# First visits of a token write its output row with the residual, second visits add to it

## The chip, the cores and the metric

The kernel runs on one core of one Trainium2 chip. The metric is the device time of one execution in microseconds (us). The kernel before took 811.41 us, the median of three runs (808.11 to 816.99). One execution of it was profiled; every row shown below comes from that one.

## The reference

One decoder layer on 1024 tokens of width 1024. The first half (attention, a linear recurrence, an output projection) gives the residual stream x. The second half routes each token to two of 32 experts, and the layer's output is x plus the gated sum of what these two experts give:

```
x  = x + gate1 * (mixed @ w_out)
h2 = rms_norm(x, norm2_g) * (1.0 + scale2) + shift2
g_p, g_idx = lax.top_k(g_prob, 1)                       # 1 of 4 groups
e_p, e_idx = lax.top_k(softmax(e_logits), TOP_K)        # 2 of its 8 experts
hid = silu(xb @ w_gate[e]) * (xb @ w_up[e])             # xb: the tokens of expert e
y   = zeros.at[row_tok].add((hid @ w_down[e]) * row_w)  # two rows are added per token
x   = x + gate2 * y
```

## The kernel before

The kernel is one program for all five engines; a scheduler puts each engine's instructions into a fixed order, in which they then run. The change touches the second half, from about 440 us of the 814.6 us span on.

**Routing.** For each pair of 128-token tiles `route` (L1273) finds the two experts of each token, and `places` (L1319) counts each token's place in its expert's list (`slot`). It turns places into lists with a product of one-hot matrices: `rec` holds for each token and choice its number and its weight, `ohs` the one-hot of the place, and `ptab` the result, a table of 32 experts by 128 places, summed up in `tb`. `h2_rows` (L1235) does two things for a tile of tokens: it writes the residual rows to the result with a DMA from the POOL queue (L1238, `out<-xr`), and the normed rows to a scratch tensor in HBM, `h2_d` (L1247).

**Units.** The expert work is cut into 20 units of up to 128 rows (`UNITS`, L73), filled in steps of 32 rows from the lists of one to four experts. Eight experts, two of each group, are fixed in advance ("front"): units 0 to 4 use only these, so their weights can be loaded before the routing is known. The other experts are ranked by their counts, and the ranking (`permi`) names the weights to load. Experts with more than 128 tokens have second and third pieces, which only units 10, 11, 14, 15 and 16 use. Lists of first pieces come from `tb`, resorted by rank (`tki`, `tkw`, L1501 to L1512); lists of further pieces come from a later pass, `overflow_tables` (L1519), which runs in small steps between the units. `pack` copies the pieces of a unit into one column of row numbers (`pki`) and weights (`pkw`).

**One unit.** For unit n the main loop (L1678) issues the loads of new experts, then the gather for unit n + 2; `gate_up` (L1642) multiplies, and in its middle the rows of unit n + 1 are transposed (`xpose`, L1604, `pxe` to `xeT`); `act` (L1620) makes `hid`; `hid_t` transposes it (`pht`, `hT`); `down` (L1653) multiplies by the third weight matrix (`py`), VectorE multiplies by `gate2` into `y` (L1663), and an indirect DMA from the POOL queue adds the rows of `y` to the rows of the result in HBM (L1665, `out<-y`, an accumulating transfer).

**Buffers and queues.** Gathered rows go to `NX` = 2 buffers (`xe`), used in turn: the gather of unit n + 2 waits until the transposes of unit n have read theirs. Expert weights are tiles of 512 KB, six per expert, 186 in all, loaded by the SP queue (L1125) into a pool of `NBLK` = 41 buffers that also holds the gate row `m_g`; a load waits for a free buffer, and for the load four places before it (`fly`). All DMA queues share the core's 16 DMA engines.

Of the kernel before, what the change touches and what calls it, by code (L numbers as in the profile page):

```python
# [26 lines left out]
NBLK = 41  # L27
BACC = dict(dynamic_dma_scratch_size=4096)
NX = 2
# [13 lines left out]
ROWS = [("gqp", 64), ("gkp", 64), ("freq", 32), ("br", 36)]  # L43
# [15 lines left out]
EBASE = {8: 1, 9: 4, 10: 7}  # L59
NST = 8  # L60
NOV = NST + 32

# [33 lines left out]
MULTI = [u for u in UNITS if len(u) > 1]  # L96
NFU = 5
GRP = [("same", 32), ("in", 4), ("by", 4), ("base", 1), ("full", 32), ("shift", 32)]
GOFF = {}
_o = 0  # L100
for _n, _w in GRP:
# [15 lines left out]
    "pt": "VS", "gl0": 6, "xa": 3, "pf": {31: 4, 32: 3, 22: 1, 25: 1, 28: 3, 7: 2, 11: 4, 12: 8, 16: 1, 17: 30}, "sqA": "G", "mg": 61, "h2p": "SSSSSSSS", "xp": "SSSSVVVV", "rh": "G", "hk": 7, "sep": 0, "rw": 2, "glw": 54, "mL": "V", "k1": 3, "gs": 1, "adv": 1, "adv0": 0, "fly": 4, "fly0": 4, "lo": "VVVG", "ptc": "SSV", "lw": 1, "lw2": 1, "lw3": 2, "lw4": 3, "ro": 0, "in_l1": "G", "xsc": "VSVSVVVV", "pin": "Y", "st": 0, "ta": 2, "sq": "SSVVSSVV", "sqL": "G",  # L117
# [21 lines left out]
def layer(ctx, tc, A, out, dbg=None, stop=None):  # L139
# [193 lines left out]
    V.tensor_scalar(tokm, tokc[:, :NT], -float(S), None, op0=OP.add)  # L333
# [840 lines left out]
    NXE = 2  # L1174
# [26 lines left out]
    rec = c2.tile([128, NT, 2, 2], F32, name="rec")  # L1201
    tb = c2.tile([128, 64], F32, name="tb")
# [32 lines left out]
    def h2_rows(t):  # L1235
        x1 = St[t]["x"]
        tsl = slice(t * 128, t * 128 + 128)
        G.dma_start(out[tsl, :], x1)  # L1238
# [80 lines left out]
    def places(g):  # L1319
# [3 lines left out]
        for a in range(2):  # L1323
            o = pp[:, a * 32:a * 32 + 32]
            T.matmul(o, tri, mb[:, a], start=True, stop=False)
            if a:
# [6 lines left out]
        V.scalar_tensor_tensor(rec[:, ts, :, 0], slot[:, ts], -1.0, tokm[:, ts, None].to_broadcast([128, 2, 2]),  # L1333
                               op0=OP.mult, op1=OP.add)
        ptab = bank("ptab")[:, :64]
        tc_ = "p t c a -> p (t c) a"
        rh = sm.tile([128, 4, 2, 32], F32, name="rhs", bufs=1)
        V.tensor_mul(rh, M[:, ts].rearrange(tc_)[:, :, None, :].to_broadcast([128, 4, 2, 32]),
                     rec[:, ts].rearrange(tc_)[:, :, :, None].to_broadcast([128, 4, 2, 32]))
        for c in range(2):  # L1340
# [3 lines left out]
            for a in range(2):  # L1344
                T.matmul(ptab, oh[:, a], rh[:, 2 * a + c].rearrange("p c e -> p (c e)"), start=(c == 0 and a == 0),
                         stop=(c == 1 and a == 1))
# [80 lines left out]
    trash = tokc[:, NT:NT + 1]  # L1427
    tk0 = c2.tile([128, 32], I32, name="tk0")
    V.tensor_scalar(tk0, tb[:, 0:32], trash, None, op0=OP.add)
# [11 lines left out]
    def column(p, m):  # L1441
        if p < NF:
            e = FRONT[p]
            return tk0[:, e:e + 1], tb[:, 32 + e:33 + e]
        if m:
            c = EBASE[p] + m - 1
            return toi[:, c:c + 1], tow[:, c:c + 1]
        return tki[:, p:p + 1], tkw[:, p:p + 1]

    def plan(u):  # L1450
        if len(u) == 1:
            i, w = column(*u[0][:2])
        else:
            c = MULTI.index(u)
            i, w = pki[:, c:c + 1], pkw[:, c:c + 1]
        n = max(g[2] + g[3] for g in u) * 32
        return i[:n], w[:n], [(0, i[:n])]

    pki = c2.tile([128, len(MULTI)], I32, name="pki")
    pkw = c2.tile([128, len(MULTI)], F32, name="pkw")  # L1460
    xrow = {0: gather(plan(UNITS[0])[0])}

    def pack(pieces):
        for c, (p, m, a, n, r) in pieces:
            i, w = column(p, m)
            V.tensor_copy(pki[32 * a:32 * (a + n), c:c + 1], i[r:r + 32 * n])
            last["pack"] = V.tensor_copy(pkw[32 * a:32 * (a + n), c:c + 1], w[r:r + 32 * n]).ins
# [210 lines left out]
    for n, u in enumerate(UNITS):  # L1678
# [4 lines left out]
        if n + 2 < len(UNITS):  # L1683
            if any(g[1] for g in UNITS[n + 2]):
                drain(tab)
# [89 lines left out]
```

## Time and profile before

| | |
|---|---|
| runs | 808.11, 811.41, 816.99 us, median 811.41 |
| profiled execution, its own time | 816.49 us |
| its span, first to last instruction | 814.6 us |
| TensorE (PE) busy | 728.1 us (89%) |
| VectorE (DVE) busy | 447.2 us (55%) |
| ScalarE (ACT) busy | 317.0 us (39%) |
| GpSimd (POOL) busy | 157.6 us (19%) |
| moved by DMA | 180.47 MB |
| expert weight loads | 186 of 512 KB, the last issued at 792.0 us |
| first product of the expert stage, last scatter | 520.5 us, 806.85 us |

The profile says of each engine when it was busy, what it waited for, and how busy the 16 DMA engines were. An engine with little idle time is not by that alone the bound: one has to see for whom the others wait in each stretch. The chain of waits in this trace holds only the last scatter and no more, so it does not answer that; the stretches do.

### The profile page before, as it was taken

The page shows a single profiled execution, that of the slowest core. Times are in us where ns is not written, and L with a number is a line of the kernel's source. Part 1 is how long each engine was busy: PE and PEld are TensorE (multiplying, and loading weights), DVE is VectorE, ACT ScalarE, POOL GpSimd, SP SyncE. Part 2 cuts the span into 40 slices and gives each one's busy share as a digit, 9 for nine tenths or more (in the row PEclk, how much of TensorE's full clock was granted, in tenths as well). Part 3 has the DMA queues.
Part 4 walks back from the last instruction along what each step waited for, and adds up shares of the span by engine and source line. Part 5 has one row for each costly group of instructions (what it writes and reads, how often), then busy time and mean ns, then how long its engine had stood idle before and what let it go on. Part 6 is the DMA issues. An engine that isn't in the chain of part 4 may idle for free. (4 is left out here: it accounts for less than half of the span.)

```text
span 814.6 us, 12260 instructions
## 1 busy us (share of the span) xinstructions
PE 728.1 (89%) x4257; PEld 471.2 (58%) x4257; DVE 447.2 (55%) x1334; ACT 317.0 (39%) x715; POOL 157.6 (19%) x150
## 2 busy tenths in 40 slices
PE   3899999989988989899999997699979899999874
PEld 1477776548877878788888886333333343332321
DVE  4597386868777469797884667344334222213210
ACT  3455456666354157667664434121201211102200
POOL 1121012103665102031311000212112112212010
PEclk9989999999999999999999998699989999999998
DMA  9952437681317403020154789999999999999994
GB/s 311 372 151 84 143 108 236 210 280 58 109 44 259 168 39 104 1 79 1 54 173 144 259 311 343 346 316 349 313 373 330 329 335 336 369 347 354 304 320 102
DMA packets 70976, 180.47 MB, mean 222 GB/s; under 512 B 8960, under 2 KB 22528, under 8 KB 70912
## 3 DMA queue, kind: packets, MB, share of 16 engines
q1 hardware_dynamic: 63328, 158.50, 55.1%
q0 software_dynamic: 7104, 21.00, 9.5%
q8 instruction: 34, 0.56, 0.3%
q10 hardware_dynamic: 480, 0.16, 0.2%
q14 instruction: 30, 0.25, 0.1%
HBM read 160.61 MB, written 22.95 MB: 225 GB/s over the span
## 5 line engine op out<-in xcount | busy, mean ns | idle before, releaser
L1649 PE MATMUL pgu<-ew,xeT 128*32 128x512 f32 (+1 forms) x928 | 163.4, 613 | 8.1 <-DMA ew<-in_w_e 7.3
L1649 PEld LDWEIGHTS pgu<-ew,xeT 128*32 128x32 f32 (+1 forms) x928 | 48.3, 121 | 99.4 <-issue 79.0
L1660 PE MATMUL py<-ew,hT 128*32 128x512 f32 (+1 forms) x464 | 75.1, 597 | 5.8 <-ACT hT L1634 5.8
L225 PE MATMUL pp<-hTh,winh 128*128 128x512 f32 x176 | 69.2, 406 | 5.8 <-DVE hTh L188 3.0
L226 PE MATMUL pp<-hTl,winh 128*128 128x512 f32 x176 | 71.1, 404 | 0.0
L227 PE MATMUL pp<-hTh,winl 128*128 128x512 f32 x176 | 70.4, 401 | 0.0
L1663 DVE TENSOR_TENSOR y<-py,m_g 128x512 f32<-128x512 f32 (+1 forms) x40 | 27.5, 691 | 69.3 <-PE py L1660 64.3
L1623 ACT ACTIVATE sg<-pgu 128x256 f32<-128x256 f32 (+1 forms) x20 | 7.7, 387 | 142.9 <-PE pgu L1649 135.8
L1660 PEld LDWEIGHTS py<-ew,hT 128*32 128x32 f32 (+1 forms) x464 | 23.5, 120 | 48.3 <-issue 35.7
L1616 DVE TENSOR_SCALAR xeT<-pxe,gc,mc 128x128 f32<-128x128 f32 x80 | 27.4, 404 | 33.0 <-PE pxe L1610 33.0
L225 PEld LDWEIGHTS pp<-hTh,winh 128*128 128x128 f32 x176 | 34.0, 194 | 16.3 <-DVE hTh L188 4.0
L1665 POOL DMA_INDIRECT out<-y,pki x13 | 20.7, 1589 | 111.2 <-DVE y L1663 87.7
L1625 DVE SCALAR_TENSOR_TENSOR hid<-sg,pkw,pgu 128x256 f32<-128x256 f32 (+1 forms) x13 | 6.2, 479 | 63.4 <-ACT sg L1623 60.9
L1634 ACT ACTIVATE hT<-pht 128x256 f32<-128x256 f32 (+1 forms) x20 | 7.6, 380 | 85.1 <-PE pht L1632 65.4
L1614 ACT ACTIVATE xeT<-pxe,mc,gc 128x128 f32<-128x128 f32 x80 | 30.0, 461 | 24.9 <-PE pxe L1610 24.9
L226 PEld LDWEIGHTS pp<-hTl,winh 128*128 128x128 f32 x176 | 33.9, 193 | 9.9 <-issue 2.1
L227 PEld LDWEIGHTS pp<-hTh,winl 128*128 128x128 f32 x176 | 34.1, 194 | 8.6 <-issue 1.7
L949 ACT ACTIVATE P<-pS,nb,scq 128x384 f32<-128x384 f32 (+2 forms) x48 | 32.3, 679 | 12.2 <-DVE nb L946 12.2
L983 PE MATMUL po<-PT,v 128*128 128x256 f32 (+1 forms) x160 | 35.8, 362 | 0.0
L1046 POOL TENSOR_TENSOR wo<-wo,m_g 128x256 f32<-128x256 f32 x32 | 28.2, 916 | 15.3 <-DMA wo<-in_w_out 15.3
L983 PEld LDWEIGHTS po<-PT,v 128*128 128x128 f32 x160 | 28.8, 191 | 2.9
L1610 PEld LDWEIGHTS pxe<-ident,xe 128*128 128x128 f32 x160 | 18.2, 145 | 20.7 <-issue 14.4
(424 smaller groups left out, 1613.6 us busy)
## 6 DMA issues: line engine op xcount, KB each, us to landing
ew<-in_w_e SPq DMA_DIRECT2D x186, 512.0 KB
wad<-in_w_ada SPq DMA_DIRECT2D x64, 256.0 KB
wada<-in_w_ada SPq DMA_DIRECT2D x16, 512.0 KB
win<-in_w_in SPq DMA_DIRECT2D x12, 512.0 KB
xt<-in_x SPq DMA_DIRECT2D x8, 512.0 KB
wo<-in_w_out SPq DMA_DIRECT2D x8, 512.0 KB
xr<-in_x SPq DMA_DIRECT2D x8, 512.0 KB
x_d<-xr SPq DMA_DIRECT2D x8, 512.0 KB
```

Of the source, the lines that this page charges most:

```text
L225: T.matmul(o, lhi, rhi, start=first, stop=False)
L226: T.matmul(o, lhi, rlo, start=False, stop=False)
L227: T.matmul(o, llo, rhi, start=False, stop=last)
L949: SC.activation(Pt[:, o:o + w], pss[ci], AF.Exp, scale=P["scq"][:, i:i + 1], bias=nb, accum_out=l[:, ci:ci + 1])
L983: T.matmul(po[:, o:], P["v"][:, js], PT[j // 4][:, j % 4, o:], start=(j == 0), stop=(j == nj - 1), skip_group_check=True)
L1046: EN[OPT["g1"]].tensor_mul(w[:, q:q + 256], w[:, q:q + 256], mrow["g1"][:, q:q + 256])
L1614: SC.activation(xT[a][:, c], pt[:, c], AF.Identity, scale=gc[:, k:k + 1], bias=sh2[:, k:k + 1])
L1616: last["dve"] = V.tensor_scalar(xT[a][:, c], pt[:, c], gc[:, k:k + 1], sh2[:, k:k + 1], op0=OP.mult, op1=OP.add).ins
L1649: T.matmul(pg[r], xT[k // 4][:, c + r.start:c + r.stop], w[k // 2][:, NS[k % 2]], start=(k == 0), stop=(k == 7), skip_group_check=True)
L1660: T.matmul(py[n][r], hT[:, a * 128 + r.start:a * 128 + r.stop], w[4 + a][:, NS[n]], start=(a == 0), stop=(a == 1), skip_group_check=True)
L1663: last["dve"] = V.tensor_mul(y[:rows, NS[n]], py[n][:rows], mrow["g2"][:rows, NS[n]]).ins
L1665: G.indirect_dma_start(out=out, out_offset=bass.IndirectOffsetOnAxis(ap=idx, axis=0), in_=y[r0:r0 + idx.shape[0]], in_offset=None, compute ...
```

## The change

Every token is visited twice. The new kernel marks for each of its two rows whether it is the earlier one in the order of the units. The earlier row is written to the result by a plain scatter, with the residual already added to it; the later one is added by an accumulating scatter.

- The eight writes of the residual (L1238) are gone. Instead `down` adds the residual to `y`: the gathered row is x times its norm factor, so x is that row times the reciprocal of the factor (`rinv`). The third value of `rec` is that reciprocal for a first visit and 0 for a second, and one more vector operation per half of `y` (L1696 of the new file) uses it.
- Each unit has three lists in place of one: `get` for the gather, `put` and `add` for the two scatters, made by four small operations (`lists`). A row that does not belong to a scatter has a number outside the result and is skipped. Unit 0 has only a `put`. The two scatters go to two views of the result that the scheduler treats as different tensors; each `add` waits for the `put` of the unit before.
- Since `y` now reads the gathered rows, their buffer is held until then: `NX` is 3, and `NBLK` is 40 in return.
- Only the front experts get their lists in `places` (8 columns of three values in place of 32 of two; four more small vector operations per pair of tiles decide who is first). The resorting (L1501 to L1512) is gone. All other units, from unit 5 on, take their lists from one late pass, `late_tables`, which is the former overflow pass with 64 columns of three values; it runs in units 0 to 2, three steps at a time, and must be done before the gather of unit 5.

```
-NBLK = 41
+NBLK = 40
-NX = 2
+NX = 3
...
     def h2_rows(t):
-        G.dma_start(out[tsl, :], x1)
...
+        V.tensor_tensor(inc, pp3, RW("cff")[:, None, :].to_broadcast([128, 2, 32]), op=OP.is_lt)
+        V.tensor_mul(scr, inc[:, :, None, :].to_broadcast([128, 2, 2, 32]), M[:, ts])
+        fst = two(2, "fst")
+        V.tensor_reduce(fst, scr, op=OP.add, axis=AX.X)
+        V.reciprocal(rinv[:, ts], ivx[:, ts])
+        V.tensor_mul(fst, fst, rinv[:, ts, None].to_broadcast([128, 2, 2]))
+        for c in range(2):
+            V.tensor_sub(rec[:, ts, c, 2], rinv[:, ts], fst[:, :, 1 - c])
...
+    def lists(c0, c1, src=None, dst=None):
...
+        V.tensor_scalar(get, v[:, :, 0], float(OOB), None, op0=OP.add)
+        V.tensor_scalar(t, v[:, :, 2], 0.0, 2.0 * OOB, op0=OP.is_gt, op1=OP.mult)
+        V.scalar_tensor_tensor(put, v[:, :, 0], 3.0 * OOB, t, op0=OP.add, op1=OP.subtract)
+        last["pack"] = V.scalar_tensor_tensor(add, v[:, :, 0], float(OOB), t, op0=OP.add, op1=OP.add).ins
...
-    pT = bank("pT")
-    for c in range(2):
-        T.transpose(pT[:32, c * 128:c * 128 + 128], tb[:, c * 32:c * 32 + 32], ident)
...
     def late_tables():
...
+        for c in range(2):
+            for t0 in range(0, NT, 2):
+                ts = slice(t0, t0 + 2)
+                oh = t3(half("oh")[:, :256], 2)
+                V.tensor_tensor(oh, iota[:, None, :].to_broadcast([128, 2, 128]),
+                                pf[:, ts, c:c + 1].to_broadcast([128, 2, 128]), op=OP.is_equal)
+                rh = half("rh")[:, :384].rearrange("p (t v e) -> p t v e", t=2, v=3)
...
+                if ready:
+                    products(*ready)
...
         for n in range(2):
-            last["dve"] = V.tensor_mul(y[:rows, NS[n]], py[n][:rows], mrow["g2"][:rows, NS[n]]).ins
...
+            V.tensor_mul(y[:rows, NS[n]], py[n][:rows], mrow["g2"][:rows, NS[n]])
+            last["dve"] = V.scalar_tensor_tensor(y[:rows, NS[n]], x[:rows, NS[n]], r, y[:rows, NS[n]],
+                                                 op0=OP.mult, op1=OP.add).ins
...
+            before = last.get("put")
+            last["put"] = scatter(seen[0], put, OP.bypass)
+            if add is not None:
+                i = scatter(seen[1], add, OP.add)
+                tc.add_manual_dep(i, before.name, mybir.DependencyInfo(
+                    mybir.DependencyClass.Sync, mybir.DependencyReason.DATA), reason="rows are written before they are added to")
...
         if n + 2 < len(UNITS):
+            while n + 2 >= NFU and done[0] < n + 3:
+                next(tab)
+            xrow[n + 2] = gather(plan(n + 2)[0])
```

The order of the instructions moves at three places of which the prediction speaks. The first is the POOL queue at the start of the expert stage. Before, the gathers (`xe<-h_d`) of units 0 to 4 stand ahead of the first scatter, then scatter and gather take turns:

```order
L1437 DMA xe<-h_d,tk_5370 128x1024
L1437 DMA xe<-h_d,pki 128x1024 x4
L1665 DMA out<-y,tk_5370 1024x1024
L1437 DMA xe<-h_d,pki 128x1024
L1665 DMA out<-y,pki 1024x1024
L1437 DMA xe<-h_d,pki 128x1024
```

In the changed kernel:

```order
L1460 DMA xe<-h_d,idx_get 128x1024 x3
L1700 DMA out<-y,idx_put 1024x1024
L1460 DMA xe<-h_d,idx_get 128x1024
L1700 DMA out<-y,idx_put 1024x1024
L1700 DMA out<-y,idx_add 1024x1024
L1460 DMA xe<-h_d,idx_get 128x1024
```

Three gathers stand ahead of the first scatter; from there on the gather of unit m stands behind the scatters of unit m - 3.

The second place is PE from the down product of unit 0 (`py`, 128x512) to that of unit 1. Before, the transposes for unit 2 (`pxe`, 7 and 1) stand here, and those for unit 3 come later:

```order
L1660 MATMUL py_5533<-ew,hT 128x512
L1649 MATMUL pgu<-ew,xeT 32x512 x17
L1610 MATMUL pxe<-ident,xe 128x128 x7
L1632 MATMUL pht<-ident,hid 128x128 x2
L1610 MATMUL pxe<-ident,xe 128x128
L1649 MATMUL pgu<-ew,xeT 32x512 x16
L1660 MATMUL py<-ew,hT 32x512 x4
```

In the changed kernel:

```order
L1692 MATMUL py_5591<-ew,hT 128x512
L1678 MATMUL pgu<-ew,xeT 32x512 x32
L1639 MATMUL pxe<-ident,xe 128x128 x8
L1661 MATMUL pht<-ident,hid 128x128 x2
L1692 MATMUL py<-ew,hT 32x512 x4
L1692 MATMUL py_5737<-ew,hT 32x512 x4
```

These eight transposes are those of unit 3. They stand ahead of the down product of unit 1, so that product waits for the gather of unit 3 too.

The third place is VectorE, from the `y` of unit 0 to the `hid` of unit 1. Before, it holds short copies of lists between them:

```order
L1663 TENSOR_TENSOR y<-py_5533,m_g_5155 128x512
L1466 COPY pki<-tki 64x1
L1467 COPY pkw<-tkw 64x1
L1466 COPY pki<-tki 32x1
L1467 COPY pkw<-tkw 32x1
```

In the changed kernel the two new operations of `y` and the late pass (`mt`, `o_...`) stand ahead of the scaled transposes of unit 2 (`xeT`):

```order
L1696 SCALAR_TENSOR_TENSOR y<-xe,pk,y 128x512
L1695 TENSOR_TENSOR y<-py_5591,m_g_5173 128x512
L1696 SCALAR_TENSOR_TENSOR y<-xe,pk,y 128x512
L1571 TENSOR_TENSOR mt<-M,fs 128x256 x3
L1645 TENSOR_SCALAR xeT<-pxe,gc,mc_349 128x128 x4
L1575 TENSOR_TENSOR o_full<-slot,o_full 128x16
L1572 TENSOR_REDUCE o_shift<-mt 128x8
```

The late pass has moved two units ahead: before, its first rows come behind the `y` of unit 1.

## Rows read from the trace of the kernel before

**Rows 1.** The page: busy tenths of the DMA engines in 40 slices.

```profile
DMA  9952437681317403020154789999999999999994
```

**Rows 2.** Stretches: PE, PEld, DVE, ACT, POOL busy; PEclk, DMA share, GB/s.

```profile
440.00:480.00 40.00, 40.00 (x239) 35.00 (x238) 22.07 (x116) 18.00 (x43) 2.93 (x5) 1.00 0.64 219
480.00:520.00 40.00, 27.62 (x187) 24.34 (x187) 25.81 (x160) 12.68 (x31) 3.70 (x5) 0.81 0.98 369
520.00:560.00 40.00, 40.00 (x274) 15.61 (x276) 15.46 (x78) 8.96 (x22) 8.25 (x7) 0.98 0.94 318
560.00:600.00 40.00, 36.62 (x297) 12.70 (x290) 18.06 (x55) 6.38 (x18) 8.00 (x7) 1.00 0.97 334
680.00:720.00 40.00, 37.02 (x199) 13.75 (x198) 10.89 (x23) 6.32 (x18) 8.67 (x7) 1.00 1.02 358
```

**Rows 3.** What the SP queue waited for, 520 to 537 us: total, times, longest.

```profile
SPq L1125 <- PE pgu L1649: 9.7, 6, 2.9
```

**Rows 4.** The same from 537 to 795 us.

```profile
SPq L1125 <- DMA ew<-in_w_e: 166.9, 135, 4.2
SPq L1125 <- PE pgu L1649: 3.5, 13, 0.4
```

**Rows 5.** Weight loads from 520 us on: count, durations in ns, first and last start.

```profile
L1125 SPq DMA_DIRECT2D ew<-in_w_e x146: 327/333/762, 523.1 to 792.0; - x146
L1125 SPq MOVE ew<-in_w_e x138: 29/29/37, 538.4 to 791.9; - x138
```

**Rows 6.** POOL's DMA queue, 480 to 509 us: packets, MB, share of 16 engines.

```profile
q0 software_dynamic: 432, 1.57, 13.3%
...
out<-xr POOLq DMA_DIRECT2D x3, 512.0 KB, 7.5
```

**Rows 7.** The same queue from 756 to 796 us.

```profile
q0 software_dynamic: 533, 1.70, 23.0%
```

**Rows 8.** Another queue, on the page, with packets of about 340 bytes.

```profile
q10 hardware_dynamic: 480, 0.16, 0.2%
```

**Rows 9.** Gathers: ns min/median/max on POOL; us from issue to landing.

```profile
L1437 POOL DMA_INDIRECT xe<-h_d,pki x13: 989/1029/1060, 512.0 to 746.5; - x13
...
DMA to landing us min/median/max: 7.7/8.0/9.9
```

**Rows 10.** Scatters on POOL, the same columns.

```profile
L1665 POOL DMA_INDIRECT out<-y,pki x13: 1475/1592/1792, 554.8 to 806.8; - x13
```

**Rows 11.** PE in order of time: start, us, instruction, count.

```profile
537.39 3.70 PE L1660 MATMUL py<-ew,hT 128*128 128x512 f32 x8
541.02 4.48 PE L1649 MATMUL pgu<-ew,xeT 128*32 128x512 f32 x34
...
550.13 3.62 PE L1660 MATMUL py<-ew,hT 128*32 128x512 f32 x32
...
563.27 3.64 PE L1660 MATMUL py<-ew,hT 128*32 128x512 f32 x32 [0.47 <-ACT hT L1634]
...
606.83 3.72 PE L1660 MATMUL py<-ew,hT 128*32 128x512 f32 x32
...
802.05 3.64 PE L1660 MATMUL py<-ew,hT 128*32 128x512 f32 x32 [0.47 <-ACT hT L1634]
```

**Rows 12.** DVE and POOL behind the last down product, in order of time.

```profile
804.92 1.52 DVE L1663 TENSOR_TENSOR y<-py,m_g 128x512 f32<-128x512 f32 x2 [3.84 <-PE py L1660]
...
806.85 1.55 POOL L1665 DMA_INDIRECT out<-y,pki  x1 [17.09 <-DVE y L1663]
```

**Rows 13.** DVE by line, 500 to 815 us: busy, mean ns, idle before.

```profile
L1663 DVE TENSOR_TENSOR y<-py,m_g 128x512 f32<-128x512 f32 x38 | 26.2, 692 | 66.0 <-PE py L1660 61.0 <-issue 4.3 <-PE pgu L1649 0.2
```

**Rows 14.** PE by line, 597 to 622 us, the same columns.

```profile
L1589 PE MATMUL pto<-ov 128*128 128x80 f32 x32 | 4.7, 302 | 2.9 <-DVE ov L1586 2.9
```

**Rows 15.** VectorE and POOL at the start of the expert stage.

```profile
510.04 0.24 DVE L1429 TENSOR_SCALAR tk<-tb,tokc 128x32 int32<-128x32 f32 x1
...
510.56 1.08 POOL L1437 DMA_INDIRECT xe<-h_d,tk  x1 [12.39 <-DVE tk L1429]
```

## What the prediction says

> **What bounds the kernel now.** I read the page's slices first, then a table of stretches, then the waits of the queue that issues the weight loads, and last PE in order of time. From 480 us almost to the end the DMA engines are full [rows 1, 2]; PE is as busy as they are only up to unit 5. So there are two candidates. The SP queue tells them apart. From 520 to 537 us its loads wait mostly for `pgu` on PE [rows 3], which means that all 41 buffers are full and PE sets the pace. From 537 to 795 us they wait 166.9 us for an earlier load and 3.5 us for PE [rows 4]: the loads run as fast as the DMA engines let them. 138 loads of ranked experts are issued from 538.4 to 791.9 us [rows 5], 253.5/138 = 1.84 us each. The last down product `py` ends at 802.05 + 3.64 = 805.69 us [rows 11], 13.7 us after the last load is issued.
>
> PE has a pace of its own that is a little faster. Its `py` ends at 541.09, 553.75 and 566.91 us [rows 11]: 12.7 and 13.2 us per unit, 12.9 in the mean. From unit 5 (`py` ends at 610.55 us) to unit 19 (805.69 us) it needs 195.14/14 = 13.94 us. The gap, 1.0 us in each of 14 units, is what the transfers hold PE up by, and all that the change can give back by relieving them.
>
> The sums below are made against the profiled run: a span of 814.6 us, 816.5 us in all. It lies 0.6% above the median of 811.41, so I multiply its totals by 811.41/816.49 = 0.9938.
>
> **What the transfers gain.** Half of the 2048 visits write plainly where before they added. Nothing in the trace writes rows plainly by an index; the nearest are the plain rows on POOL's queue, residual writes and gathers, from 480 to 509 us: 13.3% of 16 engines for 29 us are 61.7 us, over 384 rows of 4 KB 0.161 us of one engine per row [rows 6]. Where adding scatters stand beside a gather, 23.0% of 16 × 40 us are 147 us over 415 rows (1.70 MB), 0.355 us a row [rows 7]. The difference, 0.194 us × 1024 rows / 16 engines, is 12.4 us, from nothing (a put costs as much as an add) to 12.4; I take 12.4, since a put has the form of the plain rows.
>
> The eight residual writes vanish. Three of them lie in the full stretch [rows 6]: 384 × 0.161/16 = 3.9 us. I count them at nothing, because buffers are full right behind it [rows 3] and earlier loads would only wait there; the bound is −3.9. The other five lie in a stretch whose DMA share is 0.64 [rows 2], where other transfers have room. Rows that are skipped, some 2,400 more of them, are not seen apart in this trace. The cheapest packets on another queue take 0.2% × 814.6 × 16/480 = 0.054 us [rows 8]; the bounds are 0 and 2400 × 0.054/16 = 8 us, and I take 2, because a skipped row carries no data. One buffer fewer starts each load one load later: 0 to 1.84 us [rows 5], taken whole.
>
> **What the gathers lose.** This is the term against the change. `y` now reads `xe`, so the gather of unit m is released by `y` of unit m − 3 and not by transposes, and it stands on POOL behind that unit's put and add. From the end of `py(m − 3)`: 2.0 us for four operations of about 0.7, the first of which runs beside the product [rows 12, 13], 0.5 to reach POOL, the put 1.0 to 1.6 (a gather takes 1.03, a scatter 1.59 [rows 9, 10]; I take 1.3), the add 1.6, 0.6 between them, and 8.0 to land (7.7 to 9.9 [rows 9]). That is 14.0 us, from 13.4 to 16.2. Then PE may transpose unit m, and the end of `py(m − 1)` follows 12.9 us behind. So two units take at least 26.9 us, 13.45 each. In about half of the units some products stand between `py` and the transposes, which covers about 1 us of the gather and makes it 12.9. The loop runs at 13.2 us per unit, from 12.9 to 14.5. The DMA engines would allow 13.94 − (12.4 − 2)/16 = 13.3, and PE 12.9. I take 13.2.
>
> **Up to unit 5.** Before, five gathers went out ahead of all scatters and waited for nothing that was late. Now
> - the first gather is behind about six more small vector operations at 0.24 us [rows 15]: +1.4 (0 to 2.4);
> - the late pass stands on VectorE ahead of `hid` and `xeT` in units 0 to 2: +2 in unit 0 (0 to 3), from three `mt` and their like at 0.24 to 0.7 each [rows 13, 15];
> - the transposes of unit 3 stand ahead of `py(1)`. With `py(0)` at about 541.1 + 3.4 = 544.5 us, its gather is issued near 549 and lands near 557, while PE would be there at 549 to 553: +5 (4 to 8);
> - the gathers of units 4 and 5, in the same loop: +3 (0 to 6). In that wait lie the products of the tables, 4.7 us before [rows 14], now 192 columns wide in place of 80; without this cover they would cost up to 4.7 × 192/80 = 11.3 us.
>
> Together +11.4 us: `py(5)` ends near 622. The cover for the whole of this is nil, PE being busy all the time there [rows 2].
>
> **Behind the last product.** Two more operations of `y` and a second scatter in place of one. Before, the span ends 8.9 us after `py`: `y`, the issue of the scatter at 806.85 us [rows 12], and its landing. Two operations at about 0.7 less what overlaps, 1.3, and an issue of 1.6 with 0.3 between: +3.2 us. No cover: nothing else runs there.
>
> **The sum.** 610.55 + 11.4 + 14 × 13.2 = 806.8 us, against 805.7 before: +1.1. With the tail +4.3: 820.8 us for the profiled run's 816.5, or 816 on the scale of the median. What 12.4 us of transfers give back, the gathers take.
>
> **The rivals.**
> *Faster: the transfers decide.* If the gathers land early enough (7.7 us and less, as with fewer rows and a shorter queue), and PE's late start is made up from the full buffers, the end follows the last load: −12.4 + 2 + 1.8 + 1.4 + 3.2 = −4.0 us, 807.5 on the median; with the residual writes and no cost of skipped rows or of the start −12.4 − 3.9 + 1.8 + 3.2 = −11.3, 800. For it: the SP queue waits for transfers through 258 us [rows 4]. Against: PE has only 1.0 us per unit to make up 11.4 with. It decides if the loop stays under 13 us and the start under 6.
>
> *Slower: the loop of gathers binds in every unit.* Landing of 9 us and more, as the longest before [rows 9], gives (15 + 12.9)/2 = 13.9 us in each unit: 623.8 + 14 × 13.9 = 818.4, +12.7, with the tail +15.9, 827 on the median. Its place is POOL's queue, where a gather is third behind two scatters. For it: the DMA engines are full where it lands [rows 2], and it now lands beside two scatters. Against: a put is shorter than an add. It decides from a landing of about 9 us on.
>
> *The change does not do what it says.* A put costs as much as an add [rows 7], nothing is relieved, and the units keep 13.9 us: in the loads' sum 2 + 1.8 + 1.4 + 3.2 = +8.4, 820 on the median.
>
> *POOL is held up by VectorE.* The new `y` operation reads two operands in SBUF while POOL prepares scatters and gathers. Between 554.8 and 611 us scatters were issued beside such vector operations of the tables and took no more than 1.79 us [rows 10], so no row here speaks for it; if an issue took 3 us instead of 1.6, the loop would gain 4 us in two units, 15.4 us each, and the kernel 30 us.
> The Trainium skill, "SBUF — State Buffer", section "SBUF: two separate sides", states such a lock: a VectorE operation with two SBUF inputs and a GpSimd operation that reads SBUF exclude each other for the whole instruction, and a transfer issued from GpSimd can starve for its descriptors behind a VectorE copy. By that page the loss would be larger still, 620 ns becoming about 3100 (its section "A bandwidth-pool intuition that's wrong"), but the trace so far does not agree with it for these forms.
>
> **How the numbers follow.** The forecast has 0.43, the faster rival 0.27, the loop 0.24, the puts without gain 0.03, VectorE's hold 0.03. The forecast's own range is 808 (start +6, pace 13.0) to 822 (start +15, pace 13.4). About 1% is what a measurement of this kernel can tell from no change: faster is below 803.3, slower above 819.5. Of the faster rival's two ends one lies on either side of 803.3, so I put half of it, with a little of the forecast, below: 0.15. Slower are most of the loop's 0.24 (0.21), the upper end of the forecast (0.05) and most of the last two (0.04): 0.30. The rest, 0.55, is the same. The range goes from 802, between the two ends of the faster rival, to 829, a little past the loop's 827, and leaves about 1 in 10 out on either side.
>
> **What would show it.** Right: the waits of the SP queue behind 537 us move from earlier loads to `pgu` on PE; the last load is issued earlier than 792 us while `py(19)` is not; PE's `pxe` waits for transfers of `xe`, some 5 us at unit 3 near 550 to 558 us; `py(5)` ends near 622 us; the pace behind it is near 13.2 us; POOL's queue shows less than 0.355 us per row late in the stage; the span ends about 12 us behind the last `py`. Wrong: `pxe` waits for no gather (then the faster rival), or in every unit for more than 1 us (the slower one); POOL's rows cost as before; an issue on POOL takes much over 1.8 us. A low granted clock behind a new stall of PE, as the 0.81 from 480 to 520 us [rows 2], would add what none of these terms holds.

## The result and the profile after

| | before | changed |
|---|---|---|
| median of four runs each | 812.91 us | 845.97 us |
| ratio | | 1.042 (95% interval 1.034 to 1.050) |
| span of the profiled execution | 814.6 us | 843.4 us |
| end of `py` of unit 5 | 610.6 us | 628.1 us |
| end of `py` of unit 19 | 805.7 us | 831.8 us |
| from there to the end of the span | 8.9 us | 11.6 us |

The change makes the kernel 4.2% slower. Ratios leave out executions in a slower state. A ratio need not be exactly the quotient of two medians. The profiled execution of the kernel before lies 3.6 us above its median and that of the changed kernel 0.8 us below, so the two traces show 28.8 of the 33.1 us between the medians. The forecast was 816 us, no change; the measured time lies above the range (802 to 829), beyond even the slower rival, which was put at 827.

First, who waits for whom. What the SP queue waits for from 537 to 830 us, in the columns of [rows 3]:

```profile
SPq L1140 <- DMA ew<-in_w_e: 137.1, 122, 3.7
SPq L1140 <- PE pgu L1678: 18.0, 13, 6.9
SPq L1140 <- PE py L1692: 16.8, 12, 8.7
```

Before, it waited 166.9 us for earlier loads and 3.5 us for `pgu` on PE [rows 4], and for `py` as long as this row of the same view says:

```profile
SPq L1125 <- PE py L1660: 2.7, 9, 0.4
```

So its waits for these two products on PE went from 6.2 to 34.8 us: the weight buffers are full again and again, and the loads stand still because PE has not used the last ones. PE in turn, from 535 us to the end:

```profile
PE pxe L1639 <- DMA xe<-h_d,idx_get: 28.2, 8, 6.6
PE pht L1661 <- DVE hid L1654: 6.9, 5, 2.0
```

The first line did not exist before, where PE waited for no gather at all. Four of the stretches of 40 us (columns of [rows 2]):

```profile
520.00:560.00 40.00, 32.72 (x191) 14.34 (x192) 20.39 (x70) 6.74 (x16) 2.04 (x2) 0.88 0.89 319
560.00:600.00 40.00, 36.23 (x271) 13.45 (x269) 23.72 (x81) 4.72 (x13) 12.15 (x8) 0.97 0.85 288
680.00:720.00 40.00, 31.89 (x164) 13.20 (x163) 13.29 (x27) 6.88 (x19) 8.30 (x7) 0.96 0.84 306
760.00:800.00 40.00, 34.36 (x227) 11.74 (x228) 13.41 (x27) 6.63 (x19) 7.31 (x6) 0.91 0.83 290
```

PE is no longer full at the start of the expert stage (32.7 of 40 us, it was 40.0); in these four the DMA share falls to 0.83 to 0.89 where it was 0.94 to 1.02, and the granted clock of PE lies at 0.88 to 0.97. In the three stretches between them, from 600 to 680 and from 720 to 760 us, the share stays at 0.98 to 1.01. So in the four neither PE nor the DMA engines set the pace; the loop between them does. One turn of this loop in the rows, first PE (start, duration, instruction, wait before it):

```profile
680.54 3.70 PE L1692 MATMUL py<-ew,hT 128*128 128x512 f32 x8 [0.53 <-ACT hT L1663]
684.08 1.04 PE L1639 MATMUL pxe<-ident,xe 128*128 128x128 f32 x8
...
692.74 3.70 PE L1692 MATMUL py<-ew,hT 128*128 128x512 f32 x8
701.37 1.89 PE L1639 MATMUL pxe<-ident,xe 128*128 128x128 f32 x8 [4.93 <-DMA xe<-h_d,idx_get]
703.05 7.99 PE L1678 MATMUL pgu<-ew,xeT 128*128 128x512 f32 x16
710.88 0.38 PE L1661 MATMUL pht<-ident,hid 128*128 128x128 f32 x2
711.73 3.64 PE L1692 MATMUL py<-ew,hT 128*32 128x512 f32 x32 [0.47 <-ACT hT L1663]
```

then VectorE and POOL behind the first of these `py`:

```profile
684.82 0.68 DVE L1695 TENSOR_TENSOR y<-py,m_g 128x512 f32<-128x512 f32 x1
685.42 1.36 DVE L1645 TENSOR_SCALAR xeT<-pxe,gc,mc 128x128 f32<-128x128 f32 x4
686.70 0.74 DVE L1696 SCALAR_TENSOR_TENSOR y<-xe,pk,y 128x512 f32<-128x512 f32 x1
```

```profile
687.71 1.02 POOL L1700 DMA_INDIRECT out<-y,idx_put  x1 [13.08 <-DVE y L1696]
689.04 1.60 POOL L1700 DMA_INDIRECT out<-y,idx_add  x1 [0.31 <-issue]
690.94 1.05 POOL L1460 DMA_INDIRECT xe<-h_d,idx_get  x1 [0.30 <-PE pgu L1678]
```

`py` of unit 9 ends at 684.24 us. The put goes out 3.5 us later, the gather of unit 12 behind put and add at 690.94, and PE, which has reached the transposes of unit 12 at 696.4, starts them at 701.37. From there `py` of unit 11 takes until 715.37. The turn is 17.1 + 14.0 us for two units.

The same eight transposes take 1.89 us behind the wait and 1.04 us in the turn before. The granted clock (the column behind POOL's) in short stretches there:

```profile
684.00:685.20 1.20, 1.12 (x9) 0.80 (x7) 1.17 (x3) 0.48 (x2) 0.00 (x0) 1.00 1.02 413
701.30:703.00 1.70, 1.63 (x8) 1.54 (x9) 0.00 (x0) 0.56 (x2) 1.39 (x2) 0.56 1.03 415
703.00:707.00 4.00, 4.00 (x9) 1.78 (x8) 1.75 (x5) 1.23 (x4) 0.00 (x0) 0.76 1.06 341
707.00:711.00 4.00, 4.00 (x12) 1.78 (x10) 0.00 (x0) 0.00 (x0) 0.00 (x0) 1.00 0.37 110
```

Behind this wait PE ran at the lower of its two levels (1.2 in place of 2.4 GHz) for a while, and at the full one again from 707 us at the latest. The same shows behind the four longest of the eight waits, 3.8 to 6.6 us: the transposes took 1.89 to 1.97 us there. Behind the four of 1.3 to 2.9 us they took 1.09 us, as transposes do without a wait. So the long waits cost more than their length.

PE from the first transposes of the expert stage to the end of the last `py`, before and then changed:

```profile
518.70:805.70 287.00, 264.08 (x1628) 97.91 (x1628) 80.72 (x239) 44.45 (x121) 48.82 (x37) 0.98 0.96 327
```

```profile
520.10:831.90 311.80, 270.87 (x1628) 102.09 (x1628) 113.31 (x289) 44.65 (x121) 67.96 (x54) 0.94 0.85 302
```

It ran 1628 matmuls in both. It stood idle for 287.0 − 264.1 = 22.9 us before and 311.8 − 270.9 = 40.9 us after. Of the 26.1 us by which the last `py` is later, 1.4 are the later start, 18.0 are idleness, and 6.8 are PE being busy longer. Some 2 of these go to the wider tables, 6.6 us where [rows 14] had 4.7 (PE by line, columns of [rows 13]); the other 5 fit the lower clock:

```profile
L1604 PE MATMUL pto<-rh,oh 128*128 128x192 f32 x32 | 6.6, 342 | 0.0
```

### The profile page after: what moved, and what is told of

Same layout as the page of the kernel before. It is cut to its first block, busy times and chain, and to the rows that moved or that the text cites. A ratio compares the mean times of both kernels' runs of the same rounds, so it can differ in the third digit from the quotient of the medians.

```text
span 843.4 us, 12364 instructions
## 1 busy us (share of the span) xinstructions
PE 732.0 (87%) x4251; PEld 473.3 (56%) x4251; DVE 483.9 (57%) x1420; ACT 317.3 (38%) x715; POOL 174.2 (21%) x162
## 5 line engine op out<-in xcount | busy, mean ns | idle before, releaser
L1678 PE MATMUL pgu<-ew,xeT 128*32 128x512 f32 (+1 forms) x928 | 161.5, 614 | 1.2 <-ACT xeT L1643 0.5
L1692 PE MATMUL py<-ew,hT 128*32 128x512 f32 (+1 forms) x464 | 79.2, 614 | 4.4 <-ACT hT L1663 4.4
L1700 POOL DMA_INDIRECT out<-y,idx_put x20 | 20.7, 1035 | 239.7 <-DVE y L1696 198.4
L1639 PE MATMUL pxe<-ident,xe 128*128 128x128 f32 x160 | 26.4, 316 | 32.9 <-DMA xe<-h_d,idx_get 32.7
L1639 PEld LDWEIGHTS pxe<-ident,xe 128*128 128x128 f32 x160 | 20.8, 161 | 49.3 <-DMA xe<-h_d,idx_get 42.6
L1460 POOL DMA_INDIRECT xe<-h_d,idx_get x20 | 22.6, 1131 | 72.8 <-DVE cnt L1503 67.0
L964 ACT ACTIVATE P<-pS,nb,scq 128x384 f32<-128x384 f32 (+2 forms) x48 | 32.3, 680 | 12.4 <-DVE nb L961 12.0
L1700 POOL DMA_INDIRECT out<-y,idx_add x19 | 30.3, 1596 | 5.8 <-issue 5.8
```

The lines of the kernel that those rows point to most:

```text
L964: SC.activation(Pt[:, o:o + w], pss[ci], AF.Exp, scale=P["scq"][:, i:i + 1], bias=nb, accum_out=l[:, ci:ci + 1])
L1639: T.transpose(pt[:, b * 128:(b + 1) * 128], x[:, k * 128:(k + 1) * 128], ident)
L1678: T.matmul(pg[r], xT[k // 4][:, c + r.start:c + r.stop], w[k // 2][:, NS[k % 2]], start=(k == 0), stop=(k == 7), skip_group_check=True)
L1692: T.matmul(py[n][q], hT[:, a * 128 + q.start:a * 128 + q.stop], w[4 + a][:, NS[n]], start=(a == 0), stop=(a == 1), skip_group_check=True)
L1700: return G.indirect_dma_start(out=to, out_offset=bass.IndirectOffsetOnAxis(ap=ix, axis=0), in_=y[:rows], in_offset=None, compute_op=how, b ...
```

## The experiments

The theory from this profile: **the hold**. `y` keeps the gathered rows until the down product is done, the next gather into that buffer comes too late, and PE waits for it. The rivals: the new operations and the late pass themselves; the weight buffer given away.

**One gather buffer more.**

```
-NBLK = 40
+NBLK = 39
...
-NX = 3
+NX = 4
```

> The changed kernel with one gather buffer more (NX 4) and one weight buffer fewer (NBLK 39): the gather of unit m is released by y of unit m-4 and stands on POOL behind the scatters of unit m-4, one unit (12 us and more) earlier. Theory 'the loop of gathers' (PE's 28 us of waits for xe, and the low clock behind them, are the loss): the waits at pxe fall below 6 us in all, the time to 812-825 us. Rival 'late pass and small operations' (the loss lies in the tables, the lists and the two more y operations): PE still loses as much, 840 us or more. Rival 'weight buffers' (each buffer given away delays the loads): slower than the changed kernel by about 2 us, 848.

Measured: 828.75 us against 812.96 (ratio 1.020, 1.013 to 1.027). It is 17 us faster than the changed kernel, which speaks for the hold, but the waits do not vanish: 12.4 us in three places are left, and the time misses what the theory gave. The largest of them, on PE and on POOL:

```profile
623.79 1.09 PE L1639 MATMUL pxe<-ident,xe 128*128 128x128 f32 x8
630.49 1.94 PE L1639 MATMUL pxe<-ident,xe 128*128 128x128 f32 x8 [5.61 <-DMA xe<-h_d,idx_get]
```

```profile
622.08 1.05 POOL L1460 DMA_INDIRECT xe<-h_d,idx_get  x1 [0.30 <-issue]
```

These are the transposes of units 8 and 9, one behind the other. The scheduler, having one buffer more, has put the transposes of unit 9 ahead of the products of the two units before it, 7 and 8. PE takes its instructions in that order and so waits again, for a gather that was issued 8.4 us before. A later run tests that.

**The gather ahead of the scatters on POOL.** NX 3 as in the change; the gather is issued between `y` and the put.

```
+        if ahead:
+            ahead()
+
         def scatter(to, ix, how):
...
+        def ahead():
+            if n + 3 < len(UNITS) and done[0] >= n + 4:
+                xrow[n + 3] = gather(plan(n + 3)[0])
```

> The changed kernel with NX 3, but on POOL the gather of unit m stands ahead of the put and the add of unit m-3, right behind its y: 2.9 us earlier (1.0 + 0.3 + 1.6). Loop theory: each of the 8 waits of PE for xe gets up to 2.9 us shorter, 15 to 23 us in all: 823-832 us. Rival 'late pass and small operations': 843-849 us.

Measured: 828.42 us (ratio 1.019, 1.012 to 1.026), as the hold has it. PE's waits:

```profile
PE pxe L1639 <- DMA xe<-h_d,idx_get: 11.6, 6, 4.9
```

16.6 us less of waiting come with 17.5 us less of time. The gathers are issued earlier, and they also land sooner, 7.7 us behind their issue in the median where the changed kernel has 8.6. So the place behind two scatters is a good part of the loss, but not all.

**Nothing held.** The second operation of `y` is left out, and with it the residual.

```
-            V.tensor_mul(y[:rows, NS[n]], py[n][:rows], mrow["g2"][:rows, NS[n]])
-            last["dve"] = V.scalar_tensor_tensor(y[:rows, NS[n]], x[:rows, NS[n]], r, y[:rows, NS[n]],
-                                                 op0=OP.mult, op1=OP.add).ins
+            last["dve"] = V.tensor_mul(y[:rows, NS[n]], py[n][:rows], mrow["g2"][:rows, NS[n]]).ins
```

> The changed kernel without the operation that adds the residual (the output lacks it): xe is read by the transposes alone, so a gather is released by pxe of unit m-3, ahead of y. Put, add, lists and late pass stay. Loop theory: PE waits for xe under 5 us in all, 806-820 us; what is left above the kernel before is the price of the late pass. Rival 'late pass and small operations': 838-845 us, only the 1.4 us of the operation itself and a little less.

Measured: 806.01 us, ratio 0.992 (0.989 to 0.995): 0.8% faster than the kernel before, and 40 us faster than the changed one. PE waits for no gather from 535 us on; these are all its waits:

```profile
PE pht L1661 <- DVE hid L1654: 6.5, 7, 1.0
PE py L1692 <- ACT hT L1663: 5.5, 11, 0.5
```

This kernel also prices the late pass, since it has it. Its `py` of unit 5 and its last one:

```profile
605.90 3.62 PE L1692 MATMUL py<-ew,hT 128*32 128x512 f32 x32
789.04 3.64 PE L1692 MATMUL py<-ew,hT 128*32 128x512 f32 x32 [0.47 <-ACT hT L1663]
```

Unit 5 ends at 609.5 us, level with 610.6 before: the tables cost nothing by then, they are made earlier instead of between units 4 and 5. And the last one ends at 792.7 us, 13.0 earlier than in the profiled execution before; between the medians the gain is 7.0 us.

**The operation without the hold.** The new operation reads the gate row in place of `x`, so every instruction is there, and nothing holds `xe`.

```
-            last["dve"] = V.scalar_tensor_tensor(y[:rows, NS[n]], x[:rows, NS[n]], r, y[:rows, NS[n]],
+            last["dve"] = V.scalar_tensor_tensor(y[:rows, NS[n]], mrow["g2"][:rows, NS[n]], r, y[:rows, NS[n]],
```

> The changed kernel with all its instructions, but the new operation of y reads the gate row in place of the gathered rows (the output's residual is wrong): two operands in SBUF as before, nothing holds xe. It divides the 40 us between e3_no_hold (806) and the changed kernel (846) into the operation and the hold. Theory 'hold': 806-811 us, the operations cost what they add behind the last product. Rival 'VectorE's operation with two SBUF operands holds up POOL' or is itself in the way: 820 us or more, with issues on POOL over 1.8 us.

Measured: 809.61 us (ratio 0.998, 0.996 to 1.000). Of the 40 us between the kernel without the operation and the changed one, the operation costs 3.6 and the hold 36.4 by the medians. The two were measured on different chips; by the ratios, each to the kernel before on its own chip, it is 5 and 36. This kernel gives away as many weight buffers as the changed one, so that rival falls too. Its `py` of unit 5:

```profile
611.50 3.62 PE L1692 MATMUL py<-ew,hT 128*32 128x512 f32 x32
```

Scatters on POOL in this run:

```profile
L1700 POOL DMA_INDIRECT out<-y,idx_put x20: 962/1016/1386, 545.7 to 796.2; - x20
L1700 POOL DMA_INDIRECT out<-y,idx_add x19: 1485/1583/1914, 560.5 to 797.5; - x19
```

The medians are 1.02 and 1.58 us, as in the changed kernel. That alone says little of the rival that VectorE holds up POOL, because the two seldom meet: in the changed kernel no issue on POOL runs beside the new operation. Where they meet, the rows differ. In this run six gathers beside it took 0.99 to 1.06 us. With four buffers one gather took 1.51 us, and 1.44 us in the kernel with four buffers and the transposes tied, further down. Issues beside the operations of the tables, which read two SBUF operands as well, are longer; the longest of the changed kernel:

```profile
571.13 2.82 POOL L1460 DMA_INDIRECT xe<-h_d,idx_get  x1 [0.30 <-PE pgu L1678]
```

PE does not wait for this gather, which is that of unit 4. From 587 us on no issue of the changed kernel took over 1.61 us. So VectorE does not explain the waits in the loop.

**The hold in the kernel before.** The residual is written first and there is one adding scatter, as before; the buffers are held by an operation that adds zero times `xe` to `y` (`rz` holds zeros).

```
-NBLK = 41
+NBLK = 40
...
-NX = 2
+NX = 3
...
+                last["dve"] = V.scalar_tensor_tensor(y[:rows, NS[n]], x[:rows, NS[n]], rz[:rows], y[:rows, NS[n]],
+                                                     op0=OP.mult, op1=OP.add).ins
```

> The kernel before (residual written first, one adding scatter, its own tables), with the hold alone: NX 3, NBLK 40, and a second y operation that adds xe times zero, so y releases the buffer. The gather of unit m stands behind one scatter of unit m-3 instead of two, 1.3 us earlier than in the changed kernel. Loop theory: PE waits for xe at most units, 825-838 us. Rival 'late pass and small operations': 813-818 us (two operations in the tail, one buffer).

Measured: 833.53 us (ratio 1.026, 1.019 to 1.033). The hold, with the operation that makes it and one weight buffer fewer, makes the kernel before 21 us slower, without any put, list or late pass. PE waits 20.8 us for gathers; the largest line of it:

```profile
PE pxe L1610 <- DMA xe<-h_d,pki: 12.1, 5, 5.1
```

**Four buffers and the transposes tied.** As the first experiment, and PE's order is tied.

```
-                X[n + 1] = xpose(xrow[n + 1])
+                with tc.issue_after(last["pg"]):
+                    X[n + 1] = xpose(xrow[n + 1])
```

(`last["pg"]` is the last product of the first half of `gate_up`.)

> As e1_nx4, and in PE's order the transposes of unit n+1 stand behind the first half of gate_up of unit n, not ahead of it. Theory 'place of the transposes' (with NX 4 the order puts some transposes so far forward that they again wait for a gather issued only some 8 us earlier: 12.4 us of waits in 3 places, at units 7 and 13): these waits go, 808-818 us. Rival 'NX 4 costs by its weight buffers and the two y operations': stays at 826-831 us.

Measured: 812.42 us against 813.67, ratio 1.001 (0.998 to 1.005). PE's waits for gathers:

```profile
PE pxe L1639 <- DMA xe<-h_d,idx_get: 1.9, 1, 1.9
```

The whole loss is gone with one buffer and one order. So the first experiment had failed by the place of the transposes. What the weight buffers paid for it cost (39 in place of 41) is not seen apart, since this kernel also has what the puts save.

The same tie with three buffers was not run. In the changed kernel, too, transposes stand ahead of products of the unit before: those of unit 12 at 701.37 us ahead of all sixteen of unit 11, 8.0 us of work that comes only behind the wait. How much of the loss the order alone would give back is open.

**What a put saves.** The kernel that holds nothing, with the put as an adding transfer too.

```
-            last["put"] = scatter(seen[0], put, OP.bypass)
+            last["put"] = scatter(seen[0], put, OP.add)
```

> As e3_no_hold (no residual in y, nothing held), but the put is an accumulating transfer too, so half of the rows are read and written where they were written only. It prices the first term of the prediction. If a put saves 0.194 us of one engine a row, 12.4 us in all: 815-820 us (e3 took 806). If a put costs as much as an add, and e3's gain over the kernel before comes from elsewhere: 805-808 us.

Measured: 813.88 us (ratio 1.001, 0.997 to 1.004), 7.9 us more than with plain puts (7.2 by the ratios). POOL's queue on the two pages (packets, MB, share), plain puts first, adding ones second:

```profile
q0 software_dynamic: 8656, 16.82, 7.1%
```

```profile
q0 software_dynamic: 8656, 16.82, 8.6%
```

(8.6% × 813.0 − 7.1% × 802.7) × 16 = 207 us of one engine over 1024 rows: 0.20 us a row, and 12.9 us of all 16. PE waits for weights again, as in the kernel before, which it did not with plain puts:

```profile
PE pgu L1678 <- DMA ew<-in_w_e: 7.5, 5, 4.8
```

The time moved by 7.9 and not by 12.9 us, which fits that with plain puts PE, and not the loads, sets the pace for part of the stage.

**The residual writes.** The kernel before without them.

```
     def h2_rows(t):
...
-        G.dma_start(out[tsl, :], x1)
```

> The kernel before without its eight residual writes (the output lacks the residual). Prediction's step: they are worth nothing, because the weight buffers are full behind them: 811-814 us. Rival (the bound in the prediction): the loads gain 3.9 us, 808-810 us. More than 5 us would mean that the writes hold up something on POOL's queue or the gathers.

Measured: 812.17 us, ratio 1.000 (0.997 to 1.003). Its queue:

```profile
q0 software_dynamic: 5952, 16.80, 8.5%
```

They are worth nothing, as the prediction took them. Against the kernel where all scatters add, which moves as many bytes with 2704 packets more, this queue worked 1119 − 1100 = 19 us less: some 0.007 us of an engine for a skipped row; the rounding of the two shares alone can make up to 13 us of the 19.

**The residual copied early.** If `y` must not hold `xe`, its rows can be copied when they are transposed. ScalarE writes the residual into `y`, VectorE adds to it later, and NX is 2 again.

```
+    def resid(x, r):
+        n = r.shape[0]
+        y = sm.tile([128, D], F32, name="y", bufs=3)
+        SC.activation(y[:n], x[:n], AF.Copy, scale=r)
+        return y
...
+            z = half("z")
+            V.tensor_mul(z[:rows], py[n][:rows], mrow["g2"][:rows, NS[n]])
+            last["dve"] = V.tensor_add(y[:rows, NS[n]], y[:rows, NS[n]], z[:rows]).ins
```

> The changed kernel with the residual taken early: when unit n+1 is transposed, ScalarE writes its rows times the reciprocal factor into y (3 buffers), and VectorE adds the scaled product to it later (through a half tile). So xe is free after the transposes, NX is 2 again, NBLK 40. Hold theory: the time of e3_no_hold plus two vector operations at the end, 806-812 us, under the kernel before. Rival 'the new operations themselves': 825 us or more.

Measured: 835.19 us (ratio 1.026, 1.019 to 1.034), the median of three executions. The expectation failed, and the next two with it. More buffers of `y`:

```
-        y = sm.tile([128, D], F32, name="y", bufs=3)
+        y = sm.tile([128, D], F32, name="y", bufs=4)
```

(with NBLK 39; and 5 buffers with NBLK 38)

> As e7_copy (residual written into y by ScalarE at the transposes, NX 2), with 4 buffers of y in place of 3 and 39 weight buffers. In e7_copy ScalarE's copy waited 82.7 us for the adding scatter that still read the buffer, with hid and hT of other units queued behind it. Theory 'too few y buffers': one more gives a whole unit of room (12 us and more against waits of up to 16), the waits go to under 10 us, 806-812 us. Rival 'the copy itself is in the way on ScalarE': above 820 us.

> The same with 5 buffers of y and 38 weight buffers. Theory: no wait for y at all; 806-811 us if a weight buffer costs nothing, 2 to 4 us more than e9_copy4 if it costs what the prediction took for one (1.8 us).

Measured: 829.63 (ratio 1.021, 1.018 to 1.025) and 828.53 us (1.021, 1.018 to 1.024). ScalarE's longest wait in each, with 4 and with 5 buffers:

```profile
ACT y L1687 <- DMA out<-y,idx_add: 69.2, 14, 17.7
```

```profile
ACT y L1687 <- DMA xe<-h_d,idx_get: 84.9, 13, 15.7
```

With five buffers the copy no longer waits for a scatter but for the gather: it stands so early in ScalarE's order that it waits for whatever comes last, and `sg`, `hT` and the transposes' scaling stand behind it. The theory of too few buffers falls; its place in the order is left. So the copy was tied behind the scaling of its own unit:

```
+        with tc.issue_after(last["xT"]):
+            SC.activation(y[:n], x[:n], AF.Copy, scale=r)
```

> As e9_copy4, and on ScalarE each copy of rows into y stands right behind that unit's own scaled transposes, where the gather has landed for certain, not ahead of them. In e9_copy4 and e10_copy5 the copy stood ahead of them and of hT and sg of earlier units, and waited 69 to 85 us for a gather or for y, with these behind it. Theory 'place of the copy': ScalarE's waits at the copy go to under 10 us, 806-813 us. Rival 'the copy's own 1.15 us per unit on ScalarE, and fewer weight buffers': 820 us or more.

Measured: 819.58 us (ratio 1.007, 1.004 to 1.010). The waits at the copy are gone; ScalarE now waits for PE alone:

```profile
ACT hT L1663 <- PE pht L1661: 111.5, 20, 12.2
ACT sg L1652 <- PE pgu L1678: 96.1, 9, 17.1
```

The place was worth 10 us (12 by the ratios). But the time missed the 806 to 813 us of the theory: it is still 7 us over the kernel before, just under the rival's 820. PE waits 5.5 us at its transposes for VectorE's `xeT` in it, which it does in the other copying kernels and not in the changed one; whether the half tiles that `z` takes, or the copy's own time, make up the rest was not tried.

## Why the prediction was wrong

The mechanism that decided was in the prediction, and so was the view that showed it: the gather released by `y`, behind two scatters, PE waiting for it at the transposes. Its size was wrong, and with it the balance of what the gathers take and the transfers give. The forecast for the profiled run was 820.8 us and it took 845.1. Of the 24 us some 6 lie up to unit 5 and 19 in the loop behind it.

- *What the transfers gain: right.* 0.194 us a row were forecast and 0.20 measured; 12.4 us of all engines, and 12.9. (In the stretch of [rows 7] no gather was issued any more, the last went out at 746.5 us [rows 9]; so the 0.355 us are the price of an adding row without one beside it.) The writes of the residual: nothing, and nothing. Skipped rows: 2 us of 16 engines taken, about 1 measured, within the rounding. The weight buffer: 1.8 us taken; no run shows its price apart.
- *Up to unit 5: too small.* +11.4 us forecast, 628.1 − 610.6 = +17.5 measured, near the upper end of the terms' bounds. `py(0)` was foreseen at 544.5 and ended at 544.3 us; the next rows are these:

```profile
540.59 3.70 PE L1692 MATMUL py<-ew,hT 128*128 128x512 f32 x8 [0.47 <-ACT hT L1663]
...
558.05 1.97 PE L1639 MATMUL pxe<-ident,xe 128*128 128x128 f32 x8 [6.64 <-DMA xe<-h_d,idx_get]
...
560.92 3.92 PE L1692 MATMUL py<-ew,hT 128*32 128x512 f32 x32 [0.47 <-ACT hT L1663]
```

  The gather of unit 3 lands at 558 (foreseen: 557), PE waits 6.6 us for it (foreseen: 5), and the granted clock behind the wait is 0.50 from 558 to 560 us, 0.84 up to 565 and 1.00 from there. The gather of unit 5 costs another wait of 3.8 us, with 0.50 to 0.51 from 600.5 to 606 us behind it; this clock is in none of the terms. Nor do the products of the tables lie in a wait, as the prediction had them: they run from 564.8 to 578.5 us, with PE busy throughout, and take 6.6 us. The 3.4 us at unit 0, for the start and the late pass, came as 3.2, but without hold and operation they are made good by unit 5 (609.5 us against 610.6). With the operation and without the hold `py(5)` ends at 615.1 us, with both at 628.1. So the 17.5 us there are the work of the hold, 13.0 us, and of the operation, and not of the tables.
- *What the gathers lose: the step that failed.* 13.2 us per unit were forecast from unit 5 on, from 12.9 to 14.5; (831.8 − 628.1)/14 = 14.55 were measured. Two units were to take 14.0 + 12.9 us; the turn shown above took 17.1 + 14.0. Three parts of the difference are in its rows. The fourth operation of `y` came late: VectorE's order has four `xeT` of another unit (1.36 us) between the third and the fourth, so the put went out 3.5 us after `py` and not 2.5. The gather took 10.4 us to its wait's end and not 8.0. And PE's 12.9 us became 14.0, of which the eight transposes on the low clock are 0.85. This turn holds the longest of the six waits behind unit 5. In all six the way from `py` to the transposes took 13.7 to 17.1 us, 15.6 in the mean, where 14.0 were forecast. The term that was too small in every one is the landing: 8.4 to 10.6 us from the gather's issue to the end of the wait, 9.7 in the mean, for the 8.0 taken. The late fourth operation is in two of the six; in the other four the put went out 2.1 to 2.4 us after `py`. With these sizes the forecast's own sum gives (15.6 + 12.9)/2 = 14.2 us per unit. The gathers as a whole:

```profile
DMA to landing us min/median/max: 4.8/8.6/10.5
```

  The median had been 8.0 [rows 9]. The kernel with the operation and without the hold needs 12.8 us a unit there, (793.8 − 615.1)/14, close to the 12.9 of the forecast: PE's own pace was right. The estimate stood on the edge: the loop at 13.2 us beside transfers at 13.3 and PE at 12.9. It took a middle value of each bound, where a loop adds up every excess and gets nothing back for a gather that is early.
- *Behind the last product: right.* +3.2 forecast, 11.6 − 8.9 = +2.7 measured.
- *The rivals.* The faster one, −4.0 us, is what the kernel does when nothing is held: without the operation it is 7 us faster than the kernel before, with it 2 us. Its condition did not hold. The slower one had the mechanism and stopped at 827 because it took 13.9 us for the loop, out of durations at the full clock, and 623.8 − 610.55 = 13.3 us for the way up to unit 5. (The forecast has 11.4 there, and the prediction does not say where the rest comes from.) VectorE's hold on POOL did not decide: from 587 us on no issue of the changed kernel took over 1.61 us. But the prediction's "no row here speaks for it" was too strong. Its longest scatter, 1.79 us, ran beside the operations of the tables, and beside them a gather of the changed kernel took 2.82 us, and an add 3.94 us where the gather goes ahead of the scatters. The Trainium skill, "SBUF — State Buffer", section "SBUF: two separate sides", states such a lock. The runs agree with it in part: issues beside the tables' operations are longer, while beside the new operation of `y` gathers took 0.99 to 1.51 us.

The forecast named as signs of being wrong that `pxe` waits for no gather, or in every unit for more than 1 us. It was neither. Eight waits of 3.5 us in the mean, and the low clock behind four of them, were enough. It had named the clock as what none of its terms holds. One of its other signs did come, an issue on POOL of much over 1.8 us, but at the tables and at no cost to PE.

## What to carry to other kernels

When an operation late in a step begins to read an early buffer, count from that operation's end to the first instruction that needs the next contents, with issue queue, transfer and all instructions of other units that stand between, and compare it with the time that the engine has at its best; if the two are equal, the loop will lose at every excess of a transfer, and, where the wait is long enough for the clock to fall, again behind it. With one buffer more, look where the scheduler puts the in-order engine's instructions: here the fourth buffer brought 17 of 33 us by itself, and the rest only when the transposes were tied behind the first half of a unit's products. The saving of transfers was real and rightly sized, and smaller than the loss in the loop.

## What the runs showed of the hardware

- A skipped row of a scatter takes next to nothing, about 0.007 us of one engine (estimated from two pages with shares of one decimal), against 0.20 us that separate a plain row from an adding one.
- Behind waits of PE of 3.8 to 6.6 us eight transposes took 1.89 to 1.97 us, behind waits of 1.3 to 2.9 us 1.09 us. In the changed kernel's stage PE was busy some 5 us longer than before with products that had not grown, beside 18 us more of idleness.
- A gather of up to 128 rows of 4 KB kept PE waiting until 8.4 to 10.6 us behind its issue, in the six waits of the changed kernel's loop. Ahead of the two scatters the gathers landed 7.7 us behind it in the median, behind them 8.6.
